# Constants' space reused as a raw tile, six subtractions moved to VectorE, three weight fetches issued earlier

## The chip, the cores and the metric

The kernel runs on one core of a Trainium2 chip. Its engines are named as the profile names them: PE is TensorE (matmuls; PEld its weight loads), DVE is VectorE, ACT is ScalarE, POOL is GpSimd, SP is SyncE, which issues most DMAs. The metric is the device time of one execution in microseconds.

## The reference

The reference is a trunk of two layers in fp32 on one sequence of 512 tokens with 16 meta tokens ahead, 528 in all, of width 1024. Layer 0 mixes retention heads and gated DeltaNet heads, layer 1 is a Mamba-2 SSD mixer; each is followed by an MLP with squared ReLU, and after every sublayer stands a LayerNorm over alpha times the input plus the sublayer's output:

```python
def sq_relu_mlp(h, w1, w2):
    return jnp.square(jax.nn.relu(h @ w1)) @ w2
...
# every sublayer: x <- LayerNorm(alpha * x + f(x)); D_FF = 4 * 1024
```

The change lies in the two MLPs, in the norms that feed them, and in where a few constants are kept.

## The kernel before, in words

Activations stand transposed, features on partitions and tokens along the free axis, in two halves of tokens (272 and 256 in layer 0, 256 and 256 in layer 1). To get fp32 accuracy from matmuls on a reduced form, each operand is split into hi and lo: ACT casts hi (L152), DVE subtracts for lo (L153), and each product is three matmuls (L172 to L174: hh with w hi, hl with w hi, hh with w lo; or inline at L510).

Weights arrive as raw fp32 tiles of 128x1024 in a ring of twelve buffers (tag "w", `wtile`). The hi and lo tiles come from the same ring. A framework places a tile in a buffer that is free first and makes the fetch wait for the last reader of what lay there before.

A norm (`norm_after`, L325 to L341) transposes normalised rows back. For each of eight feature blocks m and both token halves hf, ACT writes hi (L337), DVE the scaled value (L339), and L340 the lo part `hl`: on DVE for m = 3 and 7, on POOL for the rest. The first matmuls of the MLP read hh and hl block by block.

An MLP (`mlp`) has eight groups of 512 hidden features. A first phase does six tiles of 128 columns in the plain way (`phase`). Thirteen `Unit`s then compute the other pairs of tiles with a Strassen-like scheme of seven products in place of eight, and between them stand `Four`s, which do the second matmul for a group. A Unit needs four blocks of w1 and four sums of them (`prepare`): the raw tiles are t1 (a11, a12), t2 and x, the last two holding a21, a22 and then the sums s1, s2, s3 (L483, L484, L486), with s4 at L487. `run` issues the seven products into three PSUM tiles ba, bb and bc (PE L510, 12 matmuls each). Between them partial sums leave PSUM into a row tile: copies on ACT (L514, L517, L520), additions on DVE (L523 for x1 += bb, L527 for x2 += ba, L531 for x3 += bc). The last product, a22, writes ba again and so has to wait for L527. Each finished quarter goes through `evac_u`: ReLU on ACT (L447), its square on POOL (L449) and on ACT (L455), the difference on DVE (L456).

The written order is the order of these generators. A scheduler of the framework then orders each engine's instructions by its own estimates of cost and readiness, so that the order on DVE, for instance, is not the written one: an instruction of a later tile can stand between two of a unit. Every engine, and SP's queue, then runs strictly in that order.

Constants of the retention heads (decay table, scalings, cosines and sines: 2088 columns) lie in one tile "cr" (DMA L1120). After retention the same space takes the final norm's weights, broadcast to all partitions (2048 columns, 1 MB, DMA L1163).

Of the kernel before, what the change touches and what calls it, by code (L numbers as in the profile page):

```python
# [12 lines left out]
F32 = mybir.dt.float32  # L13
# [5 lines left out]
P = 128  # L19
# [3 lines left out]
L = SEQ + NMETA  # L23
# [34 lines left out]
def trunk(ctx: ExitStack, tc: tile.TileContext, a, out):  # L58
# [7 lines left out]
    def nm(p):  # L66
        count[0] += 1
        return f"{p}{count[0]}"
# [59 lines left out]
    cst = one("cst", C_COLS)  # L128
    pp = one("pp", PP_COLS)
    rbc = one("rbc", 104)  # L130
    cr = sb.tile([P, R_COLS], F32, tag="cr", bufs=1, name="cr")
    ident = cst[:, C_ID:C_ID + P]
    triu = cst[:, C_TRIU:C_TRIU + P]
    ls = cst[:, C_LS:C_LS + P]
# [19 lines left out]

    def wtile(dt=F32R):
        return sb.tile([P, 1024], dt, tag="w", bufs=12, name=nm("w"))

    def fetch(src, n=1024):
        raw = wtile(F32)
# [149 lines left out]
    def norm_after(r, ns, wcol, bcol):  # L309

        res, pairs = [[], []], []
        if ns[0] + ns[1] == 512:
            res.append([])

        def task(hf):
            n, norm = ns[hf], []

            def apply(off, bn, pt, mean, rstd):
                row = tl("row", 1024)
                t2 = [row[:, j * 512:(j + 1) * 512] for j in range(2)]  # L320
                S.activation(t2[1][:bn], pt[1][:bn, :], AF.Identity, bias=shift(mean, rstd, bn), scale=rstd)
                V.tensor_scalar(t2[0][:bn], pt[0][:bn, :], mean, rstd, op0=SUB, op1=MUL)
                norm.append((off, bn, t2))

            yield from layernorm(r[hf], ns, hf, lambda: hf == 0 or len(res[0]) == KT, apply)  # L325
            yield
            for m in range(KT):
                pf = px(n)
                for off, bn, t2 in norm:
                    T.transpose(pf[:, off:off + bn], t2[m // 4][:bn, (m % 4) * P:(m % 4 + 1) * P], ident[:bn, :bn])  # L330
                if hf == 0:
                    pairs.append(htile())
                    if len(res) > 2:
                        res[2] += parts(pairs[m], [(0, 512)])
                hi, lo = parts(pairs[m], [(hf * ns[0], n)])[0]
                w, b = pp[:, wcol + m:wcol + m + 1], pp[:, bcol + m:bcol + m + 1]
                S.activation(hi, pf, AF.Identity, bias=b, scale=w)  # L337
                t = r[hf][m]
                V.tensor_scalar(t, pf, w, b, op0=MUL, op1=ADD)  # L339
                (V if m % 4 == 3 else G).tensor_tensor(lo, t, hi.bitcast(F32), op=SUB)  # L340
                res[hf].append((hi, lo))  # L341
        for hf in range(2):
            spawn(task(hf))
        return res, pairs, lambda hf: len(res[hf]) == KT
# [74 lines left out]
    def mlp(l, hx, h, ns, ready, evac0, pairs, final=None):  # L419
# [42 lines left out]
        class Unit:  # L462


            def __init__(self, c, i, evac):
                self.src = [w1[l, c * GF + i], w1[l, c * GF + i + 2]]
                self.keys, self.evac, self.ops = (i, i + 2), evac, {}
                self.gen = self.prepare()

            def prepare(self):  # L470
                t1, t2, x = fetch(self.src[0]), wtile(F32), wtile(F32)
                SY.dma_start(x[:, 0:512], self.src[1][:, 0:512])
                SY.dma_start(t2[:, 512:1024], self.src[1][:, 512:1024])
                a11, a12, s1, a22, s3, s2 = [y[:, i:i + 512] for y in (t1, t2, x) for i in (0, 512)]
                a21 = s3
                yield

                def sp(x):
                    hi, lo = tl("s", 512, F32R), tl("s", 512, F32R)
                    split(hi, lo, x)  # L480
                    return hi, lo
                s4 = tl("s", 512)
                V.tensor_tensor(s1, a21, a22, op=ADD)  # L483
                V.tensor_tensor(s3, a11, a21, op=SUB)  # L484
                yield
                V.tensor_tensor(s2, s1, a11, op=SUB)  # L486
                V.tensor_tensor(s4, a12, s2, op=SUB)  # L487
                yield
                self.ops["a11"], self.ops["a12"] = halve(t1)
                yield  # L490
                self.ops["s1"], self.ops["a22"] = halve(t2)
                yield
                self.ops["s2"] = sp(s2)
                yield
                self.ops["s3"] = sp(s3)
                yield
                self.ops["s4"] = sp(s4)
# [95 lines left out]
        for c in range(2, NG):  # L593
# [1 line left out]
        last = [four(NG - 1, 0), four(NG - 1, 1)] if final is None else [Rows()]  # L595
        gens = [st.gen for st in stages + last]
        spawn(combos(h, ns, nh, lambda: ready(1), get))
        phase([([w1[l, f]], f) for f in range(GF)], hx, groups[0][1], ns, head=3, ready=ready)
        spawn(gens[0])
        phase([([w1[l, GF + f]], f) for f in (0, 2)], hx, groups[1][1], ns)  # L600
        until(lambda: "s4" in stages[0].ops and all(x is not None for y in tt for x in y))
        B += [[half(k, 0) for k in range(4)], [half(k, 0) for k in range(4, 8)],
              [half(k, 1) for k in range(4, 8)], tt[3], tt[0], tt[1], tt[2]]
        next(gens[1])
        for i, st in enumerate(stages):
            if i + 2 < len(gens):
                next(gens[i + 2])
# [386 lines left out]
        put_fm(*done[:3], outs)  # L994
        oF[8 + 2 * hd:10 + 2 * hd] = outs

    dtab, qdec, kdec = cr[:, R_D:R_D + 512], cr[:, R_Q:R_Q + 512], cr[:, R_K:R_K + 8]
    cosT, sinT = cr[:, R_COS:R_COS + L], cr[:, R_SIN:R_SIN + L]

    def rope_tile(block, done):  # L1000
        m1, m2 = tl("s", L), tl("s", L)
# [113 lines left out]
    for hd in range(4):  # L1115
# [1 line left out]
            qF[hd] = f  # L1117
            spawn(gdn_queries(hd))
        conv_tile(a["w0"][4 + hd], gcv[4 + hd], None, done)
    SY.dma_start(cr, a["cstr"])  # L1120
    for hd in range(4):
        got = []
        for i in range(4):
# [35 lines left out]
    h = hn  # L1159


    lnf = sb.tile([P, 2048], F32, tag="cr", bufs=1, name="lnf")
    SY.dma_start(lnf, a["lnf"].unsqueeze(0).to_broadcast([P, 2048]))  # L1163
    sd = {}

    def ssd_scalars(fm):
# [234 lines left out]
    def final(u, blks, r):  # L1401


        w, b = [lnf[:, j:j + 512] for j in (0, 512)], [lnf[:, j:j + 512] for j in (1024, 1536)]

        def store(t, c0, c1, x, queue=SY):
            queue.dma_start(out[t * P:(t + 1) * P, c0:c1], x)

        def sums(t):
            pt, st = [px(512), px(512)], tl("n", 24)  # L1410
            tok = slice(t * P, (t + 1) * P)
            for j in range(2):
                for i in range(4):
                    T.matmul(pt[j][:, i * P:(i + 1) * P], r[t // 2][4 * j + i][:, t % 2 * P:t % 2 * P + P], ident,
                             start=i == 0, stop=False, is_transpose=True, skip_group_check=True)
                for k, x in enumerate(u):
                    hi, lo = blks[k][j]
                    for i, (y, z) in enumerate(((x[0], hi), (x[0], lo), (x[1], hi))):
                        T.matmul(pt[j], y[:, tok], z, start=False, stop=k == len(u) - 1 and i == 2,  # L1419
                                 skip_group_check=True)  # L1420
                for q in (2 * j, 2 * j + 1):
                    V.bn_stats(st[:, q * 6:(q + 1) * 6], pt[j][:, q % 2 * 256:q % 2 * 256 + 256])
            mv, rstd = tl("n", 2), tl("n", 1)
            V.bn_aggr(mv, g3(st, 4))
            rsq(rstd, mv[:, 1:2], 1.0, LN_EPS, 1)
            row = tl("row", 1024)
            return pt, mv[:, 0:1], rstd, row[:, 0:512], row[:, 512:1024]

        for t in range(3):
            pt, mean, rstd, t0, t1 = sums(t)  # L1430
            S.activation(t1, pt[1], AF.Identity, bias=shift(mean, rstd, P), scale=rstd)
            V.scalar_tensor_tensor(t0, pt[0], mean, w[0], op0=SUB, op1=MUL)
            V.scalar_tensor_tensor(t0, t0, rstd, b[0], op0=MUL, op1=ADD)
            store(t, 0, 512, t0)
            G.tensor_tensor(t1, t1, w[1], op=MUL)
            G.tensor_tensor(t1, t1, b[1], op=ADD)
            store(t, 512, 1024, t1)
            tick()
        with tc.manual_schedule(engines=ORDERED):
            pt, mean, rstd, t0, t1 = sums(3)  # L1440
            nb = tl("n", 1)
            V.scalar_tensor_tensor(t0, pt[0], mean, w[0], op0=SUB, op1=MUL)
            V.scalar_tensor_tensor(nb, mean, -1.0, rstd, op0=MUL, op1=MUL)
            S.activation(t1, pt[1], AF.Identity, bias=nb, scale=rstd)
            V.scalar_tensor_tensor(t0, t0, rstd, b[0], op0=MUL, op1=ADD)
            store(3, 0, 512, t0)
            G.tensor_tensor(t1[:, 0:192], t1[:, 0:192], w[1][:, 0:192], op=MUL)
            V.tensor_tensor(t1[:, 192:512], t1[:, 192:512], w[1][:, 192:512], op=MUL)
            G.tensor_tensor(t1[:, 0:192], t1[:, 0:192], b[1][:, 0:192], op=ADD)
            V.tensor_tensor(t1[:, 192:512], t1[:, 192:512], b[1][:, 192:512], op=ADD)  # L1450
            store(3, 704, 1024, t1[:, 192:512], S)
            store(3, 512, 704, t1[:, 0:192])
# [104 lines left out]
```

## Time and profile before

| what | us |
|---|---|
| timed executions, median of 3 | 1700.62 |
| lowest, highest | 1700.37, 1701.94 |
| profiled execution, its own time | 1703.35 |
| its span in the trace | 1701.6 |
| PE busy in the span | 1662.8 (98%) |
| DVE busy | 1152.1 (68%) |
| ACT busy | 739.7 (43%) |
| POOL busy | 329.4 (19%) |

The granted clock of TensorE has a mean of 0.991 of full speed. In rows of the trace a line with L is a line of the kernel before; "<-" in square brackets is the idle time of the engine ahead of an instruction and what ended it. Matmul ends overlap, so a busy PE is not PE at its peak.

### The profile page before, as it was taken

How to read it: one execution, taken by the hardware profiler on the slowest of the kernel's cores; microseconds unless marked ns; L12 is line 12 of the kernel's file. 1: busy time of each engine (PE TensorE's matmuls, PEld its weight loads, DVE VectorE, ACT ScalarE, POOL GpSimd, SP SyncE). 2: the span in 40 equal slices, each digit the busy share in tenths (PEclk: the TensorE clock that was granted, in tenths of full speed). 3: DMA queues.
4: the chain of work that ended last, by engine and by line, in shares of the span. 5: the costliest groups of instructions: out<-in, count | busy, mean ns of one | idle time of the engine just before them, and what ended most of it. 6: DMA issues, size and time to landing. Idle time of an engine off the chain costs nothing.

```text
span 1701.6 us, 29956 instructions
## 1 busy us (share of the span) xinstructions
PE 1662.8 (98%) x11884; PEld 1532.8 (90%) x11884; DVE 1152.1 (68%) x2294; ACT 739.7 (43%) x1509; POOL 329.4 (19%) x366
## 2 busy tenths in 40 slices
PE   9999999999999999999999999999999999999998
PEld 7898998899998999999998988888778888888886
DVE  6896666676437766676657776867564686777765
ACT  4432245554214534444434665756432454444441
POOL 1211210010003201111102034232410321111112
PEclk9999999999999999999999999999999999999999
DMA  6233212112221232322221443433222232322321
GB/s 217 81 101 85 72 39 80 45 63 75 87 88 56 94 100 100 100 92 89 94 78 63 127 125 106 118 112 97 84 68 100 74 101 100 100 100 100 100 100 50
DMA packets 88197, 155.60 MB, mean 91 GB/s; under 512 B 11833, under 2 KB 43193, under 8 KB 87801
## 3 DMA queue, kind: packets, MB, share of 16 engines
q1 hardware_dynamic: 87912, 153.53, 28.0%
q8 instruction: 93, 1.52, 0.4%
q14 instruction: 48, 0.39, 0.1%
q10 hardware_dynamic: 144, 0.16, 0.0%
HBM read 148.92 MB, written 4.75 MB: 90 GB/s over the span
## 4 chain that ended last, share of the span: by engine, by line
PE 81%; DVE 7%; DMA 3%; ACT 3%; POOL 3%; issue 2%; SPq 0%; POOLq 0%; DVEq 0%; ACTq 0%
PE pmm L172 18%; PE pmm L174 18%; PE pmm L173 18%; PE pmm L510 8%; PE pmx L510 6%; DVE w L153 1%; PE pmx L1419 1%; DMA w<-in_w 1%; DVE s L633 1%; DMA w<-in_mw 1%; POOL hl L340 1%; PE pmx L1273 1%; DMA row<-rd 1%; PE pmx L1277 1%; PE pmx L270 1%
## 5 line engine op out<-in xcount | busy, mean ns | idle before, releaser
L172 PE MATMUL pmm<-hh,w 128*128 128x256 f32 (+4 forms) x1480 | 456.0, 308 | 4.5 <-ACT s L626 2.6
L173 PE MATMUL pmm<-hl,w 128*128 128x256 f32 (+3 forms) x1480 | 442.3, 299 | 5.5 <-POOL hl L340 4.8
L174 PE MATMUL pmm<-hh,w 128*128 128x256 f32 (+3 forms) x1480 | 443.8, 300 | 0.2 <-DVE w L153 0.2
L152 ACT CAST w<-w 128x1024 fp32r<-128x1024 f32 (+2 forms) x253 | 261.1, 1032 | 410.9 <-PE pmm L174 170.4
L153 DVE TENSOR_TENSOR w<-w,w 128x1024 fp32r<-128x1024 f32 (+2 forms) x253 | 321.3, 1271 | 121.4 <-PE pmm L173 71.5
L172 PE MATMUL pmm<-s,w 128*128 128x256 f32 (+2 forms) x1136 | 361.5, 318 | 0.1
L174 PE MATMUL pmm<-s,w 128*128 128x256 f32 (+2 forms) x1136 | 360.9, 318 | 0.0
L173 PE MATMUL pmm<-s,w 128*128 128x256 f32 (+2 forms) x1136 | 360.4, 317 | 0.0
L172 PEld LDWEIGHTS pmm<-hh,w 128*128 128x128 f32 (+2 forms) x1480 | 279.7, 189 | 18.6 <-issue 4.5
L173 PEld LDWEIGHTS pmm<-hl,w 128*128 128x128 f32 (+1 forms) x1480 | 279.4, 189 | 17.4 <-POOL hl L340 6.1
L174 PEld LDWEIGHTS pmm<-hh,w 128*128 128x128 f32 (+1 forms) x1480 | 279.3, 189 | 8.8 <-DVE w L153 0.7
L174 PEld LDWEIGHTS pmm<-s,w 128*128 128x128 f32 x1136 | 213.8, 188 | 14.6
L172 PEld LDWEIGHTS pmm<-s,w 128*128 128x128 f32 x1136 | 213.9, 188 | 14.4 <-DVE m L381 0.3
L173 PEld LDWEIGHTS pmm<-s,w 128*128 128x128 f32 x1136 | 213.6, 188 | 14.5 <-DVE s L1352 0.3
L449 POOL TENSOR_TENSOR m<-m 128x256 f32<-128x256 f32 (+2 forms) x128 | 120.4, 943 | 512.0 <-ACT m L447 490.2
L147 POOL TENSOR_TENSOR n<-n,neg 128x1 f32<-128x1 f32 (+2 forms) x58 | 40.3, 698 | 440.3 <-DVE n L146 419.7
L633 DVE SCALAR_TENSOR_TENSOR s<-s,pp,s 128x528 f32<-128x528 f32 x120 | 101.7, 848 | 28.1 <-ACT s L631 25.9
L379 DVE TENSOR_TENSOR m<-m,pmm 128x272 f32<-128x272 f32 (+1 forms) x208 | 82.6, 416 | 19.5 <-PE pmm L174 18.8
L456 DVE TENSOR_TENSOR s<-m,s 128x256 fp32r<-128x256 f32 (+2 forms) x128 | 68.2, 535 | 28.5 <-POOL m L449 26.1
L510 PE MATMUL pmm<-s,s 128*128 128x264 f32 (+1 forms) x624 | 85.0, 286 | 2.1 <-ACT row L514 1.8
L510 PEld LDWEIGHTS pmm<-s,s 128*128 128x128 f32 x624 | 79.5, 191 | 2.7 <-ACT row L514 2.0
L1229 POOL TENSOR_TENSOR row<-row,m 128x1024 f32<-128x1024 f32 x16 | 41.0, 2564 | 112.4 <-ACT s L631 57.5
(313 smaller groups left out, 2436.4 us busy)
## 6 DMA issues: line engine op xcount, KB each, us to landing
w<-in_w SPq DMA_DIRECT2D x88, 512.0 KB, 3.3
w<-in_mw SPq DMA_DIRECT2D x172, 256.0 KB, 3.2
w<-in_mw SPq DMA_DIRECT2D x38, 512.0 KB, 3.2
w<-in_wo SPq DMA_DIRECT2D x29, 512.0 KB, 3.5
row<-rd SPq DMA_DIRECT2D x16, 512.0 KB, 5.6
s<-rd SPq DMA_DIRECT2D x32, 128.0 KB, 5.7
w<-in_w2n SPq DMA_DIRECT2D x4, 512.0 KB, 5.6
out<-row SPq DMA_DIRECT2D x7, 256.0 KB, 2.0
```

The costliest lines, as they stand in the source:

```text
L147: G.tensor_tensor(dst, t, neg5[0:part, 0:n], op=POW)
L152: S.copy(dst_hi, src)
L153: V.tensor_tensor(dst_lo, src, dst_hi.bitcast(F32), op=SUB)
L172: T.matmul(o, w[0], x[0], start=first, stop=False)
L173: T.matmul(o, w[0], x[1], start=False, stop=False)
L174: T.matmul(o, w[1], x[0], start=False, stop=last)
L379: V.tensor_tensor(t, t, o, op=ADD)
L449: G.tensor_tensor(q, t, t, op=MUL)
L456: V.tensor_tensor(lo, q, hi.bitcast(F32), op=SUB)
L510: T.matmul(o, w[x][:, c], B[b][k][y], start=first and k == i == 0, stop=last and k == 3 and i == 2, skip_group_check=True)
L633: V.scalar_tensor_tensor(acc, cin[:, k:k + L], w[k], acc, op0=MUL, op1=ADD)
L1229: G.tensor_tensor(g3(rw, 8), g3(rw, 8), bm(cb, 8), op=MUL)
```

## The change

Three edits. First, "cr" is cut into "cra" (decay table and scalings, 1032 columns) and "crb" (cosines and sines, 1056), each with a DMA of its own. After retention both serve as the third raw tile x of a Unit (`spare`): "cra" for units with i = 0, "crb" for i = 1; x no longer comes from the ring. At the end the final norm fetches its weights into "cra" and its biases into "crb" (two broadcasts of 512 KB), and the broadcast of 1 MB goes. Second, in the norm's second token half the subtraction L340 of m = 5 and 6 goes from POOL to DVE. There are three such norms, so six instructions move. Third, in an MLP's first phase the fourth tile's fetch stands right behind the third's, and the fetch of the first `Four`'s two raw tiles stands ahead of the last tile of the phase rather than behind the phase.

```diff
--- before.py
+++ after.py
@@ -128,7 +128,7 @@
     cst = one("cst", C_COLS)
     pp = one("pp", PP_COLS)
     rbc = one("rbc", 104)
-    cr = sb.tile([P, R_COLS], F32, tag="cr", bufs=1, name="cr")
+    cra, crb = one("cra", R_COS), one("crb", 2 * L)
     ident = cst[:, C_ID:C_ID + P]
     triu = cst[:, C_TRIU:C_TRIU + P]
     ls = cst[:, C_LS:C_LS + P]
@@ -154,6 +154,10 @@
 
     def wtile(dt=F32R):
         return sb.tile([P, 1024], dt, tag="w", bufs=12, name=nm("w"))
+
+    def spare(tag):
+
+        return sb.tile([P, 1024], F32, tag=tag, bufs=1, name=nm("sp"))
 
     def fetch(src, n=1024):
         raw = wtile(F32)
@@ -337,7 +341,7 @@
                 S.activation(hi, pf, AF.Identity, bias=b, scale=w)
                 t = r[hf][m]
                 V.tensor_scalar(t, pf, w, b, op0=MUL, op1=ADD)
-                (V if m % 4 == 3 else G).tensor_tensor(lo, t, hi.bitcast(F32), op=SUB)
+                (V if m % 4 == 3 or hf == 1 and m > 4 else G).tensor_tensor(lo, t, hi.bitcast(F32), op=SUB)
                 res[hf].append((hi, lo))
         for hf in range(2):
             spawn(task(hf))
@@ -464,11 +468,11 @@
 
             def __init__(self, c, i, evac):
                 self.src = [w1[l, c * GF + i], w1[l, c * GF + i + 2]]
-                self.keys, self.evac, self.ops = (i, i + 2), evac, {}
+                self.keys, self.evac, self.ops, self.tag = (i, i + 2), evac, {}, "cr" + "ab"[i]
                 self.gen = self.prepare()
 
             def prepare(self):
-                t1, t2, x = fetch(self.src[0]), wtile(F32), wtile(F32)
+                t1, t2, x = fetch(self.src[0]), wtile(F32), spare(self.tag)
                 SY.dma_start(x[:, 0:512], self.src[1][:, 0:512])
                 SY.dma_start(t2[:, 512:1024], self.src[1][:, 512:1024])
                 a11, a12, s1, a22, s3, s2 = [y[:, i:i + 512] for y in (t1, t2, x) for i in (0, 512)]
@@ -595,13 +599,26 @@
         last = [four(NG - 1, 0), four(NG - 1, 1)] if final is None else [Rows()]
         gens = [st.gen for st in stages + last]
         spawn(combos(h, ns, nh, lambda: ready(1), get))
-        phase([([w1[l, f]], f) for f in range(GF)], hx, groups[0][1], ns, head=3, ready=ready)
+        ahead = []
+
+        def third():
+            blks = wload(w1[l, 2])
+            ahead.append(fetch(w1[l, 3]))
+            return blks
+
+        phase([([w1[l, 0]], 0), ([w1[l, 1]], 1), ([third], 2), ([lambda: halve(ahead[0])], 3)], hx, groups[0][1], ns,
+              head=3, ready=ready)
         spawn(gens[0])
-        phase([([w1[l, GF + f]], f) for f in (0, 2)], hx, groups[1][1], ns)
+
+        def second():
+            blks = wload(w1[l, GF + 2])
+            next(gens[1])
+            return blks
+
+        phase([([w1[l, GF]], 0), ([second], 2)], hx, groups[1][1], ns)
         until(lambda: "s4" in stages[0].ops and all(x is not None for y in tt for x in y))
         B += [[half(k, 0) for k in range(4)], [half(k, 0) for k in range(4, 8)],
               [half(k, 1) for k in range(4, 8)], tt[3], tt[0], tt[1], tt[2]]
-        next(gens[1])
         for i, st in enumerate(stages):
             if i + 2 < len(gens):
                 next(gens[i + 2])
@@ -994,8 +1011,8 @@
         put_fm(*done[:3], outs)
         oF[8 + 2 * hd:10 + 2 * hd] = outs
 
-    dtab, qdec, kdec = cr[:, R_D:R_D + 512], cr[:, R_Q:R_Q + 512], cr[:, R_K:R_K + 8]
-    cosT, sinT = cr[:, R_COS:R_COS + L], cr[:, R_SIN:R_SIN + L]
+    dtab, qdec, kdec = cra[:, R_D:R_D + 512], cra[:, R_Q:R_Q + 512], cra[:, R_K:R_K + 8]
+    cosT, sinT = crb[:, 0:L], crb[:, L:2 * L]
 
     def rope_tile(block, done):
         m1, m2 = tl("s", L), tl("s", L)
@@ -1117,7 +1134,8 @@
             qF[hd] = f
             spawn(gdn_queries(hd))
         conv_tile(a["w0"][4 + hd], gcv[4 + hd], None, done)
-    SY.dma_start(cr, a["cstr"])
+    SY.dma_start(cra, a["cstr"][:, 0:R_COS])
+    SY.dma_start(crb, a["cstr"][:, R_COS:R_COLS])
     for hd in range(4):
         got = []
         for i in range(4):
@@ -1159,8 +1177,6 @@
     h = hn
 
 
-    lnf = sb.tile([P, 2048], F32, tag="cr", bufs=1, name="lnf")
-    SY.dma_start(lnf, a["lnf"].unsqueeze(0).to_broadcast([P, 2048]))
     sd = {}
 
     def ssd_scalars(fm):
@@ -1401,7 +1417,11 @@
     def final(u, blks, r):
 
 
-        w, b = [lnf[:, j:j + 512] for j in (0, 512)], [lnf[:, j:j + 512] for j in (1024, 1536)]
+        w, b = [], []
+        for i, (dst, tag) in enumerate(((w, "cra"), (b, "crb"))):
+            x = spare(tag)
+            SY.dma_start(x, a["lnf"][i * 1024:(i + 1) * 1024].unsqueeze(0).to_broadcast([P, 1024]))
+            dst += [x[:, 0:512], x[:, 512:1024]]
 
         def store(t, c0, c1, x, queue=SY):
             queue.dma_start(out[t * P:(t + 1) * P, c0:c1], x)
```

Lines behind the new function `spare` are four higher than before (L523 becomes L527, L527 becomes L531), and more further down. The matmuls are the same in number and shape.

**DVE in a unit.** These are the rows of DVE at the start of one usual unit's additions, in the middle of the first MLP. L523 adds bb to x1 in the tile "row", L527 adds ba to x2, L531 adds bc to x3; L456 is the difference of the squares; L153 on a tile w of 128x1024 is the lo part of a weight tile. Before:

```order
L523 TENSOR_TENSOR row_8378<-row_8378,pmx_8376 128x264
L527 TENSOR_TENSOR row_8378<-row_8378,pmm_8375 128x264
L456 TENSOR_TENSOR s_8444<-m_8441,s_8443 128x264
L456 TENSOR_TENSOR s_8465<-m_8462,s_8464 128x264
L531 TENSOR_TENSOR row_8378<-row_8378,pmx_8377 128x264
L487 TENSOR_TENSOR s_8525<-w_8369,w_8372 128x512
L153 TENSOR_TENSOR s_8595<-w_8372,s_8594 128x512
L153 TENSOR_TENSOR w_8559<-w_8369,w_8558 128x1024
```

And in the change (L527, L531 and L535 are the additions, L460 the difference):

```order
L527 TENSOR_TENSOR row_8380<-row_8380,pmx_8378 128x264
L153 TENSOR_TENSOR w_8561<-w_8371,w_8560 128x1024
L460 TENSOR_TENSOR s_8446<-m_8443,s_8445 128x264
L531 TENSOR_TENSOR row_8380<-row_8380,pmm_8377 128x264
L535 TENSOR_TENSOR row_8380<-row_8380,pmx_8379 128x264
L460 TENSOR_TENSOR s_8467<-m_8464,s_8466 128x264
```

The lo part of the next unit's first tile has moved up from behind the third addition to between the first two, and the first difference stands ahead of the second addition. So it is in 11 units of each MLP; the last unit of each had this order before. On PE one matmul of the `Four` behind stands ahead of the last product in all of them.

**DVE in the norm.** The second token half of the norm ahead of the first MLP, from the subtraction of m = 3 on; L404 is a difference for the Strassen sums. Before:

```order
L340 TENSOR_TENSOR hl_6410<-m_5894,hh_6409 128x256
L339 TENSOR_SCALAR m_5392<-pmx_6594,pp 128x256
L339 TENSOR_SCALAR m_5398<-pmx_6600,pp 128x256
L339 TENSOR_SCALAR m_5404<-pmx_6606,pp 128x256
L404 TENSOR_TENSOR m_6617<-m_5525,m_5473 128x256
L340 TENSOR_TENSOR hl_6446<-m_5404,hh_6445 128x256
```

And in the change:

```order
L344 TENSOR_TENSOR hl_6412<-m_5896,hh_6411 128x256
L343 TENSOR_SCALAR m_5394<-pmx_6596,pp 128x256
L343 TENSOR_SCALAR m_5400<-pmx_6602,pp 128x256
L344 TENSOR_TENSOR hl_6430<-m_5394,hh_6429 128x256
L344 TENSOR_TENSOR hl_6439<-m_5400,hh_6438 128x256
L343 TENSOR_SCALAR m_5406<-pmx_6608,pp 128x256
L408 TENSOR_TENSOR m_6619<-m_5527,m_5475 128x256
L344 TENSOR_TENSOR hl_6448<-m_5406,hh_6447 128x256
```

The two subtractions of m = 5 and 6 stand behind their scaled values and ahead of the scaled value of m = 7.

**DVE in the first unit.** The rows around the first addition of the first MLP's first unit; w_7265, w_7267 and sp_7268 are the raw tiles of the next unit, w_7040 a raw tile of the first `Four`. Before:

```order
L153 TENSOR_TENSOR w_7168<-w_7124,w_7167 128x1024
L523 TENSOR_TENSOR row_7136<-row_7136,pmx_7134 128x264
L527 TENSOR_TENSOR row_7136<-row_7136,pmm_7133 128x264
L456 TENSOR_TENSOR s_7202<-m_7199,s_7201 128x264
L483 TENSOR_TENSOR w_7265<-w_7266,w_7265 128x512
```

And in the change:

```order
L153 TENSOR_TENSOR w_7170<-w_7040,w_7169 128x1024
L460 TENSOR_TENSOR s_7073<-m_7105,s_7072 128x256
L153 TENSOR_TENSOR s_7126<-s_7028,s_7125 128x512
L487 TENSOR_TENSOR w_7267<-sp_7268,w_7267 128x512
L527 TENSOR_TENSOR row_7138<-row_7138,pmx_7136 128x264
L488 TENSOR_TENSOR sp_7268<-w_7265,sp_7268 128x512
L153 TENSOR_TENSOR w_7286<-w_7129,w_7285 128x1024
L460 TENSOR_TENSOR s_7204<-m_7201,s_7203 128x264
L531 TENSOR_TENSOR row_7138<-row_7138,pmm_7135 128x264
```

The next unit's sums s1 and s3 (L483 and L484 before, L487 and L488 now) have moved ahead of the first and the second addition. The second half of w_7267 is fetched into the buffer of w_7040.

## The prediction

> **What bounds the kernel now.** I read the page first, then the waits of TensorE, then the order of time around those waits. The page:
>
> ```profile
> span 1701.6 us, 29956 instructions
> PE 1662.8 (98%) x11884; PEld 1532.8 (90%) x11884; DVE 1152.1 (68%) x2294; ACT 739.7 (43%) x1509; POOL 329.4 (19%) x366
> ```
>
> TensorE is busy for 98%, and the change leaves its matmuls as they are. So the time moves only by the idle stretches of TensorE, those that go and those that come, and by the clock it is granted. The waits of TensorE that the change can touch (us in total, times, longest):
>
> ```profile
> PE pmm L173 <- POOL hl L340: 4.8, 2, 2.4
> ...
> PE pmm L510 <- ACT row L514: 1.8, 1, 1.8
> ...
> PE pmm L510 <- DVE m L379: 1.1, 2, 1.0
> ...
> PE pmm L510 <- DVE row L527: 1.0, 2, 0.5
> ```
>
> Of 26 units only two wait for L527, about 0.5 us each. The granted clock is the third number from the end of each row here, for stretches of 5 us:
>
> ```profile
> 550.00:555.00 5.00, 4.13 (x22) 4.14 (x23) 3.78 (x13) 2.04 (x6) 2.01 (x3) 0.66 0.33 111
> ...
> 580.00:585.00 5.00, 3.78 (x18) 3.78 (x19) 1.72 (x2) 1.83 (x4) 0.00 (x0) 0.66 0.75 276
> 1355.00:1360.00 5.00, 3.52 (x17) 3.52 (x18) 3.81 (x11) 2.68 (x9) 2.57 (x3) 0.66 0.21 68
> ```
>
> Behind each of the three longest waits above the clock falls to 0.66 over 5 us: 0.34 x 5 = 1.7 us of full clock missing, some of it in the idle time itself. I price a wait of about 2 us with 1.5 us on top.
>
> **Gain 1: shares in the norm.** Ahead of the first MLP:
>
> ```profile
> 546.42 1.44 DVE L339 TENSOR_SCALAR m<-pmx,pp 128x256 f32<-128x256 f32 x3
> 547.78 0.41 DVE L404 TENSOR_TENSOR m<-m,m 128x256 f32<-128x256 f32 x1
> ...
> 549.81 0.42 DVE L153 TENSOR_TENSOR s<-m,s 128x264 fp32r<-128x264 f32 x1
> 546.17 4.64 POOL L340 TENSOR_TENSOR hl<-m,hh 128x256 fp32r<-128x256 f32 x3
> 550.87 0.58 PE L173 MATMUL pmm<-hl,w 128*128 128x256 f32 x1 [2.39 <-POOL hl L340]
> L340 POOL TENSOR_TENSOR hl<-m,hh x36: 727/758/3055, 528.6 to 1353.4; 128x256 fp32r<-128x256 f32 x24, 128x272 fp32r<-128x272 f32 x12
> ```
>
> POOL's third subtraction stretched from a median of 0.758 us to 3.055: it ended at 550.81, only when VectorE's string of two-input operations (547.78 to 550.23) was over. In the change m=5 and 6 stand on VectorE behind the second of the three L339 (ends 547.4): at 0.34 us from start to start, as in the string above, they are done near 547.8 and 548.2. The last L339 then ends near 548.6, and m=7, behind one L404, near 549.3 instead of 548.5. TensorE would wait some 0.3 + 0.6 us instead of 0.2 + 2.4. That is 1.7 us, and 1.5 of clock, since 0.6 is short of what lowered it: 3.2 us. The second MLP's start has the same wait (2 x 2.4 = 4.8 above) and the same clock: 6.4 together. Bounds: 3.4 (clock not regained) to 7.8 (no wait left).
>
> By the Trainium skill, TensorE: Matmul & The Clock Gate, section "What's actually happening", the clock halves only after an idle window of some 3.4 us; then waits of 2.4 us would cost nothing on top, and the 4.5 us of clock in my gains would not come back. The three rows with 0.66 speak against it, so the measurement decides; it is a rival below.
>
> **Gain 2: the second matmul's first weights.** In the first unit of the first MLP:
>
> ```profile
> 574.55 3.19 SPq L549 DMA_DIRECT2D w<-in_mw  x6
> 579.85 1.04 ACT L152 CAST w<-w 128x1024 fp32r<-128x1024 f32 x1 [1.04 <-DMA w<-in_mw]
> 580.80 0.37 ACT L514 COPY row<-pmm 128x264 f32<-128x264 f32 x1
> 581.22 2.83 PE L510 MATMUL pmm<-s,s 128*128 128x264 f32 x12 [1.80 <-ACT row L514]
> ```
>
> The cast of a raw tile asked for at about 575 waits for the DMA; the copy L514 that TensorE needs is queued behind it. In the change these two tiles are asked for before the last phase tile, some 20 us earlier, and the wait goes: 1.8 + 1.5 = 3.3 us (bounds 1.8 and 3.3). The two waits for L379 (1.1) may shrink too; I count 0.5. Gains: about 10.2 us.
>
> **Loss 1: the order inside a unit.** Each unit takes one tile less from the ring of 12, and the scheduler now puts the lo part of its first tile (L153, 128x1024) between L523 and L456, and L456 ahead of L527. A unit of before that has its usual order:
>
> ```profile
> 641.94 1.05 ACT L152 CAST w<-w 128x1024 fp32r<-128x1024 f32 x1 [1.07 <-PE pmx L510]
> 642.01 0.43 DVE L523 TENSOR_TENSOR row<-row,pmx 128x264 f32<-128x264 f32 x1 [2.23 <-PE pmx L510]
> ...
> 643.40 0.63 POOL L449 TENSOR_TENSOR m<-m 128x264 f32<-128x264 f32 x1 [16.11 <-ACT m L447]
> ...
> 643.47 0.43 DVE L527 TENSOR_TENSOR row<-row,pmm 128x264 f32<-128x264 f32 x1 [1.03 <-PE pmm L510]
> ...
> 644.65 0.52 PE L510 MATMUL pmm<-s,w 128*128 128x264 f32 x3
> ```
>
> Matmuls of this size follow each other by 0.12 us (0.52 for three, the last 0.28 long). L527 is over at 643.90, and the unit's last product (a22, which overwrites the PSUM that L527 reads) starts at 644.65 without a wait. The last unit of the same MLP already has the new order:
>
> ```profile
> 863.11 1.05 ACT L152 CAST w<-w 128x1024 fp32r<-128x1024 f32 x1 [0.97 <-PE pmx L510]
> 863.31 0.43 DVE L523 TENSOR_TENSOR row<-row,pmx 128x264 f32<-128x264 f32 x1 [4.43 <-PE pmx L510]
> ...
> 864.19 1.23 DVE L153 TENSOR_TENSOR w<-w,w 128x1024 fp32r<-128x1024 f32 x1 [0.46 <-ACT w L152]
> ...
> 864.56 1.34 POOL L449 TENSOR_TENSOR m<-m 128x264 f32<-128x264 f32 x1 [16.01 <-ACT m L447]
> ...
> 865.94 0.43 DVE L456 TENSOR_TENSOR s<-m,s 128x264 fp32r<-128x264 f32 x1 [0.52 <-POOL m L449]
> 865.95 0.28 PE L172 MATMUL pmm<-s,w 128*128 128x272 f32 x1
> 866.29 0.42 DVE L527 TENSOR_TENSOR row<-row,pmm 128x264 f32<-128x264 f32 x1
> ...
> 866.77 0.63 PE L510 MATMUL pmm<-s,w 128*128 128x264 f32 x3 [0.54 <-DVE row L527]
> ```
>
> L153 waits for its cast and runs to 865.42. POOL's L449 takes 1.34 instead of 0.63 beside it and ends 0.48 behind it. L456 waits for POOL, L527 stands behind L456, and a22 behind L527: it starts at 866.77 instead of one matmul (0.12) after 865.95, 0.70 late, and the refill behind the wait costs another 0.1: 0.8 us.
>
> For a unit as at 642: the cast ends at 642.99, L153 runs 643.02 to 644.25, POOL ends near 644.73, L456 starts at 644.76, L527 at 645.11, a22 at 645.59. One matmul of the other product stands ahead of a22 there, so it is late by 645.59 - 644.77 = 0.82, with the refill 0.92. The second MLP:
>
> ```profile
> 1462.24 1.05 ACT L152 CAST w<-w 128x1024 fp32r<-128x1024 f32 x1 [1.05 <-PE pmx L510]
> ...
> 1464.87 0.53 PE L510 MATMUL pmm<-s,w 128*128 128x256 f32 x3
> ```
>
> The same steps from the cast's end at 1463.29 put a22 at 1465.86, against 1464.87 and one matmul of the other product, twice as wide there, so about 0.22: 0.77, with refill 0.88. Eleven units of each MLP change to this order: 11 x 0.92 + 11 x 0.88 = 19.8 us. Nothing covers it, as TensorE works in order and waits nowhere else in a unit; these stretches are too short to lower the clock (0.54 us above did not: the unit at 863 shows matmuls 0.12 us apart on both sides). Bounds per unit: 0.5 (the wait at its shortest in the rows) to 1.1 (POOL started its whole 0.63 after L153).
>
> By the Trainium skill, SBUF — State Buffer, section "Who interferes with whom", a GpSimd operation that reads SBUF is blocked outright while a VectorE operation with two SBUF inputs runs. Then POOL's 0.63 would start when L153 ends, 0.15 later than the row has it (0.48), and 22 units would cost 3 us more; the row is used.
>
> **Loss 2: the first unit of each MLP.** In the first MLP, s1 of the next unit (L483; L487 in the change) now stands ahead of L523, L484 and an L153 behind it. It needs a transfer into the buffer of the second matmul's second raw tile, which is free only when that tile is split.
>
> ```profile
> 575.93 0.68 DVE L487 TENSOR_TENSOR s<-w,w 128x512 f32<-128x512 f32 x1
> 576.53 1.28 DVE L153 TENSOR_TENSOR s<-w,s 128x512 fp32r<-128x512 f32 x2
> ...
> 586.04 0.43 DVE L523 TENSOR_TENSOR row<-row,pmx 128x264 f32<-128x264 f32 x1 [3.89 <-PE pmx L510]
> 1387.59 0.42 DVE L523 TENSOR_TENSOR row<-row,pmx 128x256 f32<-128x256 f32 x1 [0.91 <-PE pmx L510]
> w<-in_mw SPq DMA_DIRECT2D x172, 256.0 KB, 3.2
> ```
>
> These three and two splits of a whole tile (1.23 each, row 864.19) end near 580.4; the transfer lands 3.2 later, and s1 takes 0.68: near 584.3. Without the 3.3 of gain 2's wait, L523 was due at 582.7 (it started at 586.04): 1.6 late. With L484 (0.6) besides and the order of loss 1, a22 comes some 2.2 us late. A wait of 1.8 lowered the clock, so half of 1.5 is added: 3 us, bounds 0.9 and 5.5. In the second MLP all three sums stand ahead of its first L523: 3 x 0.68 less the 0.91 that VectorE idles ahead of it (the last row), and 0.88 as in loss 1: 2 us, bounds 0.9 and 5.
>
> **Nothing else is priced.** The two fetches into the spare tile that now stand early in SP's queue wait for retention's last reads; the first of them, of cosines and sines, is this one:
>
> ```profile
> L1006 DVE TENSOR_TENSOR s<-pmm,cr x16: 402/415/431, 90.2 to 194.3; 128x272 f32<-128x272 f32 x8, 128x256 f32<-128x256 f32 x8
> ```
>
> The weight fetch queued behind it leaves about a microsecond later, and is covered by the tile that TensorE is working on; the other stands where the 1 MB fetch stood. Were that cover gone, each would cost 1 to 2 us. The final norm's fetches land long before their use.
>
> **The sum.** -6.4 - 3.3 - 0.5 + 19.8 + 5 = +14.6 us, rounded to +14 on the profiled execution's 1703.35 us (1701.6 of span and 1.75 around it). That execution is 2.7 above the median of the runs; on 1700.62 it gives **1714 us**.
>
> **The rivals.**
> - *The units don't wait.* If L153's string is not the one that holds L527, only the gains are left: 1700.6 - 10.2 + 2 = 1692.4. For it: most idle time of VectorE lies in the same units (2.23 us ahead of L523 at 642). Against it: the row at 866.77, and the same order of rows. 0.14.
> - *A draw.* A wait of 0.5 per unit, as the shortest row (11 us), first units of 2, gains of 10: 1700.6 - 10.2 + 13 = 1703.4, or 1701.4 with the gains at their upper bound (12.2). 0.12, of which 0.09 lie within 0.2%.
> - *The first units stall on the transfers.* Landing behind other fetches, both lose 5 us and the half clock: 1714 + 6 = 1720. Among the rows there, 3.2 is a median; 579.85 came 5 us after its issue. 0.12.
> - *The clock isn't regained*, being set by something else than these waits: 1714 + 4.5 = 1718.5. 0.07.
> - *The forecast itself*, 1706 to 1718: 0.55.
>
> Changes within 0.2% (3.4 us) can't be told from none here. Faster 0.15, the same 0.09, slower 0.76. The range reaches from 1696 to 1722; the likeliest case's own is 1706 to 1718.
>
> **What would show it.** Right: TensorE's waits for L527 (L531 in the change) rise from two to about 24 with some 0.7 us each, POOL's L449 has 20 more with 1.3 us, the waits for POOL's L340 and for L514's copy are gone, and no stretch at 550, 580 and 1355 has a clock of 0.66. Wrong: L527 starts within 2 us of L523 in the units, or a wait for a DMA stands behind each unit's first sum.

## The result and the profile after

The changed kernel is slower, by 0.77%:

| | median, us | range, us | runs |
|---|---|---|---|
| before | 1700.49 | 1695.86 to 1702.44 | 6 |
| changed | 1713.67 | 1710.59 to 1716.13 | 6 |

The ratio is 1.0077, with a 95% interval from 1.0063 to 1.0092: 10.7 to 15.6 us more. The profiled execution of the change took 1710.59 us, the least of its six, while that of before (1703.35) lies above all six of its kernel; so the two traces differ by less than the medians, by 7.2 us of span. From the page of the change:

```profile
span 1708.8 us, 29912 instructions
PE 1662.7 (97%) x11884; PEld 1529.0 (89%) x11884; DVE 1154.1 (68%) x2300; ACT 739.0 (43%) x1509; POOL 316.9 (19%) x360
```

TensorE is busy for as long as before (1662.8), so the longer span is idle time of TensorE. The waits of TensorE in the change (us in total, times, longest):

```profile
PE pmm L514 <- DVE row L531: 14.5, 26, 2.1
...
PE pmm L176 <- ACT m L451: 1.8, 2, 0.9
...
PE pmm L177 <- DVE hl L344: 0.9, 2, 0.5
```

L531 is the addition x2 += ba (L527 before): two waits of 1.0 us in all have become 26 of 14.5. The wait for POOL's subtraction (4.8) and the one for ACT's copy (1.8) are gone; two waits of 0.9 us for L451, the ReLU that empties a PSUM tile, are new. A usual unit, in order of time:

```profile
639.51 1.05 ACT L152 CAST w<-w 128x1024 fp32r<-128x1024 f32 x1 [0.96 <-PE pmx L514]
639.70 0.43 DVE L527 TENSOR_TENSOR row<-row,pmx 128x264 f32<-128x264 f32 x1 [4.40 <-PE pmx L514]
...
640.60 1.23 DVE L153 TENSOR_TENSOR w<-w,w 128x1024 fp32r<-128x1024 f32 x1 [0.47 <-ACT w L152]
...
640.96 1.34 POOL L453 TENSOR_TENSOR m<-m 128x264 f32<-128x264 f32 x1 [17.31 <-ACT m L451]
...
642.34 0.43 DVE L460 TENSOR_TENSOR s<-m,s 128x264 fp32r<-128x264 f32 x1 [0.52 <-POOL m L453]
642.69 0.42 DVE L531 TENSOR_TENSOR row<-row,pmm 128x264 f32<-128x264 f32 x1
...
643.17 0.51 PE L514 MATMUL pmm<-s,w 128*128 128x264 f32 x2 [0.55 <-DVE row L531]
```

This is the order of the unit at 863 in the kernel before, step for step: POOL's square stretched to 1.34 us beside VectorE's lo part, the difference behind POOL, the addition behind the difference, and the last product 0.55 us late. Units start 22.70 us apart in the first MLP (first additions at 617.00 and 639.70) in place of 21.90 (620.11 and 642.01), and 21.79 in place of 21.08 in the second: 0.80 and 0.71 us each.

How much longer or shorter each stretch of the program became can be read from the starts of the same matmuls in both traces. Worked out so, with the stretches named by their times in the kernel before:

| stretch of before, us | what lies there | change, us |
|---|---|---|
| 0 to 535 | layer 0's mixer | -0.6 |
| 535 to 565 | norm, first phase | -0.8 |
| 565 to 585 | the copy in the first unit | -3.6 |
| 585 to 600 | rest of the first unit | +1.9 |
| 600 to 905 | units 2 to 13 of the first MLP | +6.6 |
| 905 to 1330 | a norm and layer 1's mixer | -4.1 |
| 1330 to 1366 | norm | -0.5 |
| 1366 to 1400 | first phase, first unit | +0.5 |
| 1400 to the end | the rest of the second MLP | +7.7 |

The stretches of the two MLPs and the norms ahead of them make +11.8, near the +13.2 of the medians. Of the 4.1 us in the mixer's stretch, 2.5 are chance: the execution of before waited 1.84 us at 1157 and had the half clock behind it, that of the change waited 0.95 and did not. About 0.6 us, from 920 to 950, lie at the third norm, whose two subtractions moved as well; the kernels below show 0.5 there with this edit (e3, e5) and none without it (e2, e4). The rest was not traced. Single traces of the other kernels stand between -4.6 and +2.5 in the whole stretch. So totals are taken from the timed runs, and traces only say where.

### The profile page after: what moved, and what is told of

The parts are those of the page before. It is cut to its first block, busy times and chain, and to the rows that moved or that the text cites. A ratio compares the mean times of both kernels' runs of the same rounds, so it can differ in the third digit from the quotient of the medians.

```text
span 1708.8 us, 29912 instructions
## 1 busy us (share of the span) xinstructions
PE 1662.7 (97%) x11884; PEld 1529.0 (89%) x11884; DVE 1154.1 (68%) x2300; ACT 739.0 (43%) x1509; POOL 316.9 (19%) x360
## 4 chain that ended last, share of the span: by engine, by line
PE 81%; DVE 8%; ACT 3%; POOL 3%; issue 2%; DMA 2%; SPq 0%; POOLq 0%; DVEq 0%; ACTq 0%
PE pmm L178 19%; PE pmm L177 19%; PE pmm L176 19%; PE pmm L514 7%; PE pmx L514 4%; POOL m L453 2%; ACT w L152 1%; DVE w L153 1%; PE pmx L1439 1%; DVE s L650 1%; DMA w<-in_w 1%; PE pmx L1289 1%; ACT m L451 1%; DVE s L460 1%; PE pmx L1293 1%
## 5 line engine op out<-in xcount | busy, mean ns | idle before, releaser
L176 PE MATMUL pmm<-hh,w 128*128 128x256 f32 (+5 forms) x1480 | 455.2, 308 | 5.6 <-ACT s L643 2.0
L153 DVE TENSOR_TENSOR w<-w,w 128x1024 fp32r<-128x1024 f32 (+2 forms) x253 | 312.3, 1236 | 147.7 <-PE pmm L177 79.8
L152 ACT CAST w<-w 128x1024 fp32r<-128x1024 f32 (+2 forms) x253 | 260.9, 1032 | 347.5 <-PE pmm L177 88.9
L460 DVE TENSOR_TENSOR s<-m,s 128x256 fp32r<-128x256 f32 (+2 forms) x128 | 64.9, 508 | 43.9 <-POOL m L453 41.5
L527 DVE TENSOR_TENSOR row<-row,pmx 128x264 f32<-128x264 f32 (+1 forms) x26 | 11.0, 424 | 97.2 <-PE pmx L514 97.2
```

Source lines behind the costliest of these rows:

```text
L152: S.copy(dst_hi, src)
L153: V.tensor_tensor(dst_lo, src, dst_hi.bitcast(F32), op=SUB)
L176: T.matmul(o, w[0], x[0], start=first, stop=False)
L460: V.tensor_tensor(lo, q, hi.bitcast(F32), op=SUB)
```

## Experiments

All ratios are to the kernel before on the same chip, with 95% intervals. e1 to e4, e5 to e7 and e8 to e10 each ran together; the median of before from those runs stands at the first of each group.

| kernel | median, us | ratio |
|---|---|---|
| e1: the change, ring of 11 | 1695.77 (before 1699.58) | 0.9979 (0.9969 to 0.9989) |
| e2: spare tiles alone | 1717.58 | 1.0109 (1.0093 to 1.0125) |
| e3: norm's shares alone | 1699.29 | 0.9997 (0.9984 to 1.0010) |
| e4: three fetches alone | 1698.42 | 0.9999 (0.9990 to 1.0008) |
| e5: shares and fetches | 1694.52 (before 1702.84) | 0.9957 (0.9939 to 0.9974) |
| e6: e5, sums two steps later | 1696.47 | 0.9961 (0.9947 to 0.9975) |
| e7: the change, square on ACT | 1695.91 | 0.9967 (0.9954 to 0.9981) |
| e8: before, square on ACT | 1693.07 (before 1702.56) | 0.9955 (0.9939 to 0.9971) |
| e9: e5, square on ACT, sums one step later | 1684.47 | 0.9897 (0.9879 to 0.9915) |
| e10: the change, both of these | 1692.00 | 0.9939 (0.9921 to 0.9957) |

**e1: one buffer less.** If the order in the units is the cause, and the order came from the freed buffers of the ring, taking one buffer away should give the old order back with all else as in the change.

```diff
-        return sb.tile([P, 1024], dt, tag="w", bufs=12, name=nm("w"))
+        return sb.tile([P, 1024], dt, tag="w", bufs=11, name=nm("w"))
```

> The whole change, with a ring of 11 weight buffers in place of 12; the additions of a unit then stand in their old order on VectorE (x1 += bb directly ahead of x2 += ba) in 25 of 26 units, while the spare tiles and all fetches stay as in the change. Theory A (the order inside the unit costs the time): TensorE waits for x2 += ba in at most 2 units instead of 26, and about 17 us come back: 1694 to 1698 us, 3 to 6 us below the kernel before. Rival B (the fetches into the spare tiles and the first units' transfers cost it): the ring is tighter, so nothing comes back: 1713 or more.

It took 1695.77 us, as theory A had it. TensorE's waits in e1:

```profile
PE pmm L176 <- ACT m L451: 1.8, 2, 0.9
...
PE pmm L514 <- DVE row L531: 0.4, 1, 0.4
```

One wait for x2 += ba is left of 26, with the same spare tiles and fetches, and in 25 units x2 += ba stands directly behind x1 += bb on VectorE again. Rival B is out: more room cost the time, and less room won it back.

**e2: the spare tiles alone.** L340 and the phases are as before; the rest of the change stays. The diff is against the change, and shortened.

```diff
-                (V if m % 4 == 3 or hf == 1 and m > 4 else G).tensor_tensor(lo, t, hi.bitcast(F32), op=SUB)
+                (V if m % 4 == 3 else G).tensor_tensor(lo, t, hi.bitcast(F32), op=SUB)
...
+        next(gens[1])
         for i, st in enumerate(stages):
```

> Only the spare tiles and the final norm's weights in them; the norm's shares and the three fetches as before. Theory A: every unit has the new order, 11 x 0.80 + 11 x 0.76 = 17 us, and little at the first units, so 1716 to 1719 us, with 24 or more waits for x2 += ba of 0.45 us and more. Rival B: 1700 to 1705, since without the moved fetches the first units have no late transfer.

1717.58 us, 1.09% more, within what theory A said. Its waits:

```profile
PE pmm L514 <- DVE row L531: 12.9, 26, 0.6
PE pmm L177 <- POOL hl L344: 6.0, 2, 3.0
```

All 26 units wait, and none longer than 0.6 us: without the moved fetches the first unit has no wait of 2.1. The spare tiles hold the whole loss in the time, and the rest of the change is a gain.

**e3 and e4: the two other edits, one by one.** The diffs are those lines of the change.

> Only the norm's shares: m = 5 and 6 of the second token half on VectorE. Theory A: the wait for POOL goes, but the next tile's matmuls wait for ACT's ReLU that empties a PSUM tile, which is queued behind two casts and runs at the same time as before; 0.8 us at each of two norms and no clock regained: 1698 to 1700 us, and a stretch of 5 us with a clock of 0.66 behind both. Rival (the prediction's price): 6.4 us and no such stretch: 1694.

> Only the three fetches moved up. Theory A: the wait of the first unit for ACT's copy goes, with the clock behind it: 3.3 us, so 1697 us, VectorE's order in the units as before. Rival: the transfers collide with the phase's own and a wait for a DMA shows up there: 1700 to 1703.

Neither can be told from before. In e3 the wait for POOL is gone, and in its place stands

```profile
PE pmm L172 <- ACT m L447: 1.8, 2, 0.9
```

as theory A said. The half clock that it expected behind both norms came behind the first alone (0.72 over 550 to 555, 1.00 over 1355 to 1360).

What neither theory had is the wait for ACT's copy in the first unit. It is gone in e3's trace, and in e2's and e8's, which touch neither the norm nor these fetches. In e4, which has only the moved fetches, 0.8 us of it stays at 579.65, and in e5 below 1.0. So theory A of e4 was wrong in its wait, and this wait was not the fetches' own to win. What in the timing sets it off was not traced.

**e5: both together, no spare tiles.**

> The norm's shares and the three fetches, without the spare tiles. Theory A (the order inside the units is the whole loss, and the rest of the change gains what its traces showed, where the wait for ACT's copy in the first unit goes with either edit alone): as with the ring of 11, 1694 to 1698 us, no wait for POOL's subtraction, none for the copy, two waits for x2 += ba. Rival: the gains of the two edits add up as predicted, 9.7 us: 1690.

1694.52 us, 0.43% less (0.26 to 0.61). The time fits theory A, and so do the wait for POOL, which is gone, and the two waits left for x2 += ba; the wait for the copy does not, as 1.0 us of it stays. The two edits alone gave nothing that could be told and together 7 us; the intervals of e3 and e4 reach down to 0.16 and 0.10%, so they may add up, and this stays open.

**e6: what the norm's gain ran into.** In the change ACT's queue behind the norm looks like this, with TensorE's next wait:

```profile
548.25 0.41 ACT L152 CAST s<-m 128x264 fp32r<-128x264 f32 x1 [2.29 <-DVE m L408]
549.25 0.41 ACT L152 CAST s<-m 128x264 fp32r<-128x264 f32 x1 [0.60 <-DVE m L408]
549.57 0.39 ACT L451 ACTIVATE m<-pmm 128x272 f32<-128x272 f32 x1
```

```profile
550.01 0.38 PE L176 MATMUL pmm<-hh,w 128*128 128x256 f32 x1 [0.91 <-ACT m L451]
```

Two casts of Strassen sums wait for VectorE's differences, and the ReLU that frees the PSUM tile stands behind them. In the kernel before it ran at the same time, hidden under the wait for POOL, which ended at 550.81:

```profile
549.55 0.39 ACT L447 ACTIVATE m<-pmm 128x272 f32<-128x272 f32 x1
```

e6 is e5 with the sums beginning two steps later.

```diff
         yield from wait(go)
+        yield from pause(2)
         for k in range(4):
```

> As the kernel with the norm's shares and the three fetches, and the Strassen sums of the activations (their casts on ACT stood ahead of the first ReLU that empties a PSUM tile) begin two steps later, so that two ReLUs stand ahead of those casts. Theory C (behind the wait for POOL stood a second one, for that ReLU, due at the same time, which is why the norm's shares gave 0.8 us and no clock): the two waits of 0.9 us for ACT's ReLU go, and the half clock behind the norms with them: 2 x (0.9 + 1.5) = 4.8 us less than without it, about 1691. Rival: the clock is set by the idle time of the norm itself and the sums then come late at the first unit: within 1 us of the kernel without it, with a wait for the sums at the first unit.

1696.47 us, no less than e5. In the trace both parts happened. The waits for the ReLU are gone from both norms, and the clock stays whole there; but TensorE then waits at the first units, in the first MLP for ACT's copy and in the second for a cast:

```profile
PE pmm L511 <- ACT row L515: 2.3, 1, 2.3
PE pmm L511 <- ACT s L152: 1.4, 1, 1.4
```

```profile
550.00:555.00 5.00, 5.00 (x44) 5.00 (x43) 4.97 (x15) 3.64 (x10) 1.25 (x2) 1.00 0.48 162
575.00:580.00 5.00, 3.12 (x15) 3.12 (x16) 2.94 (x4) 2.42 (x6) 1.25 (x1) 0.72 0.38 121
```

Against e5's trace the stretches of the norms are some 1.4 and 3.2 us shorter, and those of the first units 2.8 and 1.7 us longer. The copy starts no earlier than in e5 (576.46 against 576.45), so TensorE, which comes earlier, waits for it. Theory C names the wait at the norm rightly; its price for the kernel was wrong, since the first units took back what the norms gave, as its rival had it.

**e7 and e8: POOL's part in a unit's stall.** The square moves from POOL to ACT, in the change (e7) and, as a control, in the kernel before (e8).

```diff
-                G.tensor_tensor(q, t, t, op=MUL)
+                S.activation(q, t, AF.Square)
```

> The whole change, with the square of the evacuations (L453) computed by ACT instead of POOL; VectorE's order is the new one in 24 of 26 units. Theory D (POOL's square, blocked while the lo part of a whole weight tile runs on VectorE, holds the difference and with it x2 += ba): the difference starts directly behind that lo part, some 0.5 us earlier, the wait for x2 += ba falls from 0.5 to 0.1 us or less, and the kernel takes 0.4 to 0.6 us less per unit: 1700 to 1705. Rival: the lo part alone holds the additions, and POOL is not what they wait for: waits of 0.5 us as before, 1712 to 1715.

> The kernel before with the square of the evacuations on ACT: the control for the change with the same edit. VectorE's order is the old one in 24 of 26 units. Theory D (the edit helps the change because it frees the difference from POOL) : there is nothing to free here beyond the last unit of each MLP, so 1698 to 1702, within 3 us of before. Rival E (the square on ACT is faster by itself, whatever the order): some 17 us less here too, about 1685.

A unit of e7, which has the new order:

```profile
639.79 1.23 DVE L153 TENSOR_TENSOR w<-w,w 128x1024 fp32r<-128x1024 f32 x1 [0.47 <-ACT w L152]
640.11 0.43 ACT L453 ACTIVATE m<-m 128x264 f32<-128x264 f32 x1
...
640.93 0.43 DVE L460 TENSOR_TENSOR s<-m,s 128x264 fp32r<-128x264 f32 x1
641.28 0.42 DVE L531 TENSOR_TENSOR row<-row,pmm 128x264 f32<-128x264 f32 x1
641.53 0.29 PE L176 MATMUL pmm<-s,w 128*128 128x272 f32 x1
...
641.76 0.64 PE L514 MATMUL pmm<-s,w 128*128 128x264 f32 x3
```

The difference starts directly behind the lo part (at 640.93, where the lo part's row ends at 641.02), without the 0.52 us of waiting for POOL, and the last product starts without a wait, though L531 is still behind L153 and L460. In the whole of e7 one wait for x2 += ba is left, of 1.3 us in the first unit. So the stall needs both: the lo part ahead of the addition, and POOL held up by it.

The time fell by more than expected, to 1695.91. The control says why: the square on ACT takes 0.45% off the kernel before as well (0.29 to 0.61, some 7.6 us), where theory D had no more than 3 us and rival E 17. The ratios of the control can't simply be subtracted, as 3.6 us of its gain are the wait for the copy in the first unit, which the change had already lost. So the stretches of the later units are compared, as in the table above: e7's are 7.1 and 7.3 us shorter than the change's in the two MLPs, e8's 2.2 and 1.0 us shorter than before's. The difference, some 11 us or 0.5 for each of 22 units, belongs to the stall. Theory D holds for the stall, but had no price for the edit itself. e7's units start 22.09 us apart where before had 21.90, so 0.2 us stay without any wait that the profile lists.

**e9 and e10: a faster kernel.** Both have the square on ACT and `pause(1)` in place of e6's `pause(2)`; e9 has no spare tiles.

> The norm's shares, the three fetches, the square on ACT, and the Strassen sums one step later (one ReLU ahead of their casts in place of none); no spare tiles. Theory C: the first wait for ACT's ReLU behind the norm goes, the sums are late by less than with two steps: 1688 to 1693. Rival: as with two steps, what goes at the norm comes back at the first unit: 1694 to 1697.

> The whole change with the square on ACT and the Strassen sums one step later; VectorE's new order stays in 23 of 26 units. By theory D the units cost at most 0.1 us each, so this should lie within 3 us of the same kernel without the spare tiles: 1688 to 1696. Rival: the new order still costs 0.5 us or more per unit, so 10 us more than without the spare tiles.

e9 takes 1684.47 us, 1.0% less than before and the fastest of all. In it neither a norm nor a first unit lowers the clock, and TensorE has no idle time in these stretches:

```profile
545.00:550.00 5.00, 5.00 (x43) 4.89 (x42) 5.00 (x13) 3.76 (x9) 3.01 (x4) 1.00 0.16 54
550.00:555.00 5.00, 5.00 (x45) 5.00 (x44) 4.07 (x15) 3.39 (x10) 0.00 (x0) 1.00 0.43 157
575.00:580.00 5.00, 5.00 (x43) 5.00 (x42) 2.73 (x5) 2.92 (x6) 0.00 (x0) 1.00 0.48 157
...
1340.00:1345.00 5.00, 5.00 (x43) 4.89 (x43) 4.77 (x14) 2.06 (x7) 0.66 (x1) 1.00 0.10 36
```

Against before, the stretches of the two norms are 4.2 and 4.4 us shorter in e9, and in e8, which has the square on ACT alone, they are as long as before to 0.1 us. So the gain that the prediction looked for at the norms was there, once the ReLU no longer stood behind the casts.

e10 takes 7.5 us more than e9. Theory D had at most 3, its rival 10, and the intervals of the two ratios leave room for both. The traces show some 0.12 and 0.18 us per unit (22.11 against 21.99 apart, 21.24 against 21.06), a little over theory D's 0.1 and far from its rival's 0.5. That makes 3.3 us in all, and a wait of 0.93 in the first unit comes on top; the rest is not located. Even then the spare tiles gain nothing.

## Why the prediction was right, and where it was not

The forecast was 1714 us and slower; 1713.67 were measured, and the mechanism of the loss is the one that the runs show: the order inside a unit, passed on by POOL's square. That the number came out to a third of a microsecond is luck. The gains and the losses were both too large, and the sum was rounded down on the way: +14.6 on 1700.62 is 1715.2.

- **Loss 1, the order in a unit: right, a little too large.** Predicted were 0.92 and 0.88 us per unit, 19.8 in all; usual units show 0.80 and 0.71, 16.6. The step that was off is the cast's place: I took it from the unit at 642, where it starts 0.07 us ahead of the first addition. In the change it starts 0.19 ahead, about as in the unit at 863 (0.20), so everything behind it comes 0.12 earlier. e1 and e2 show that the order is the cause, and e7 that POOL's square is what passes the delay on. The signs came as described: 26 waits, and 25 squares of 1.33 to 1.35 us on POOL in place of 2. The waits are 0.5 us each, not 0.7, but a wait of the list counts from the end of the matmul ahead, 0.29 us after its start, where the next one would have followed after 0.12; so the unit loses more than the list says.
- **Loss 2, the first units: right in the first MLP, too large in the second.** The wait for the transfer came as described:

```profile
578.45 0.33 SPq L477 DMA_DIRECT2D w<-in_mw  x1
```

```profile
582.10 0.69 DVE L487 TENSOR_TENSOR w<-sp,w 128x512 f32<-128x512 f32 x1 [2.74 <-DMA w<-in_mw]
582.71 0.42 DVE L527 TENSOR_TENSOR row<-row,pmx 128x264 f32<-128x264 f32 x1
```

  s1 of the next unit waits 2.74 us for a fetch issued at 578.45, and x1 += bb stands behind it. TensorE then waits 2.1 us, with no half clock behind it (1.00 over 585 to 590, in the rows below); the stretch cost 1.9 in place of 3. In the second MLP it was 0.5 in place of 2: the wait there is 0.5 us, like any unit's.
- **Gain 1, the norm's shares: the step that failed.** 6.4 us were predicted, 3.4 the lower bound; the trace shows 0.8 and 0.5. POOL's wait went as described, and TensorE's own wait for VectorE's subtraction is 0.5 us, near the 0.6 forecast. What I did not look for is what stood behind it: ACT's ReLU, which starts at 549.55 before and at 549.57 in the change, and for which TensorE now waits 0.9 us. The 1.5 us of clock at each norm did not come back either in this trace. The price of 1.5 for a wait of about 2 us does not hold in general: behind the waits of 2.40 us in e4 and 2.98 in e2 at the first norm the clock was 1.00. The third norm, priced at nothing, gave some 0.6. In the change the clock still falls behind both norms ahead of an MLP (first and last row):

```profile
550.00:555.00 5.00, 4.99 (x29) 4.99 (x30) 4.46 (x13) 3.46 (x9) 1.91 (x2) 0.66 0.30 104
580.00:585.00 5.00, 4.12 (x34) 3.90 (x33) 2.77 (x4) 2.00 (x4) 1.28 (x1) 1.00 0.26 80
585.00:590.00 5.00, 3.79 (x31) 3.79 (x32) 4.30 (x8) 4.57 (x10) 2.81 (x4) 1.00 0.18 60
1355.00:1360.00 5.00, 4.11 (x22) 4.10 (x22) 4.49 (x12) 3.65 (x9) 1.79 (x2) 0.66 0.30 108
```

- **Gain 2, the copy in the first unit: right in size, wrong in owner.** 3.3 us were predicted and 3.6 show in the trace, clock included (580 to 585 is whole now). But e2, e3 and e8 lose the same wait without the moved fetches, and e4, with them alone, keeps 0.8 us of it and gains nothing that can be told. The two waits for L379 (1.1 us), counted with 0.5, are gone in the change, which lies in the +6.6 of the table; they are gone in e2 and e8 too and stay in e4 and e5, so they weren't the fetches' to win either.
- **The totals.** Gains of 10.2 us were predicted; e1 shows 3.6 and e5 7.3, by their ratios. Losses of 24.8 were predicted; e2 shows 18.5, and the change against e5 20.4. The errors, 3 to 7 and 4 to 6, cancel.
- **The rivals.** That the units don't wait (0.14) falls with the 26 waits. The draw (0.12) had the wait of 0.5 us right, but took it for a unit's whole loss, which is 0.80 and 0.71. That the clock isn't regained (0.07) came true in part, behind both norms and not in the first unit, and gave no more than a shift inside the range. That both first units stall on transfers (0.12) came true in the first, without the half clock.

## What to carry to other kernels

Room that a change frees is also given to the scheduler: a buffer more in a ring can let a long piece of prefetch work slip between two short instructions that the critical engine waits for, so compare the order on the waiting engines before and after, and try the change with the ring shortened by what it freed. Where a unit of the old trace already shows the new order, its wait is the price, and better than one pieced together. When a wait is taken away, look up when the next thing was due that the engine needs, as it may have stood under the same wait all along.

## What the runs showed of the hardware

- Less idle time can lower TensorE's clock than I had priced: after two waits of 0.47 and 0.91 us, 1.4 in all within 3 us, the change has a clock of 0.66 over 5 us, as before after 2.39. A single wait of 2.1 us in its first unit left the clock at 1.00, and so did the waits of 2.40 us in e4 and 2.98 in e2 at the first norm. The same pair of waits at the norms lowered the clock at one norm and not at the other in e1, e3, e5 and e7. So what counts here isn't one wait's length. By the Trainium skill, TensorE: Matmul & The Clock Gate, section "What's actually happening", the half clock comes after at least one idle window of about 3.4 us, and the window is free-running. That the same waits differ from run to run would fit a window that runs by itself; the amount does not fit, since in the 3.4 us ahead of the change's half clock (547.2 to 550.6) TensorE was busy for 2.0. What exactly is counted was not tried.
- POOL's square of 128x264 takes 0.63 us alone and 1.34 beside a VectorE operation of 1.23 with two inputs; it ends 0.47 us behind that operation (642.30 against 641.83). By the Trainium skill, SBUF — State Buffer, section "Who interferes with whom", the GpSimd operation is blocked outright meanwhile; the rows agree but for 0.16 us of its 0.63: only 0.47 are left when VectorE's operation ends. On ACT the same square takes 0.43 beside the same operation.
